# First modulation loaded alone, seven of eight cache samples compressed beside the projections: a prediction for one decoder step

## The chip, the cores and the metric

One core of one Trainium2 chip runs the whole program in one launch. The metric is device time in microseconds (us), the median of several executions. The engines are called PE (TensorE), DVE (VectorE), ACT (ScalarE), POOL (GpSimd) and SP (SyncE, which here only issues transfers). They run on their own and wait for one another by semaphores; each works through its own list of instructions in order.

## What is computed

One step of a hybrid decoder layer: 512 prompt tokens and 8 sampled tokens go through attention with three branches, a gated linear recurrence (HGRN) and a mixture of experts. What matters here is the start of the layer. A vector `c` per sequence gives six modulations, the input is normed and modulated, and projected:

```python
sh_a, sc_a, gt_a, sh_f, sc_f, gt_f = adaln(c, w_ada[l], b_ada[l])   # silu(c) @ w_ada + b_ada
h = rms_norm(x, g_pre_mix[l]) * (1.0 + sc_a) + sh_a
parts = split_projection(h @ w_in[l])
```

Each of the 8 samples also has a cache of 1024 rows in pages, found by a page table, which the compressed branch squeezes by a small two-layer network. That needs neither the modulation nor the projections:

```python
past_c = pool_c[page_table].reshape(b, past, NSA_KV_GROUPS, 2, NSA_HEAD_DIM)
hid = hid + jnp.einsum('bnsgkd,ksde->bngke', ch[:, r:r + n_cmp], w1r[:, r])
return jnp.einsum('bngke,kef->bngkf', jax.nn.gelu(hid), w2)
```

## The kernel before

The 520 tokens are columns of 128-row tiles; D = 1024 makes KT = 8 slices. Four pieces of work make up the start.

**The normed input.** `normed(t)` loads a tile of 128 tokens on ACT's queue, norms it on ACT and DVE, and transposes it on PE (L356) into `xnT`.

**The first modulation.** `ada(0, ...)` multiplies silu(c) (`sT`) with 8 slices of `wa`, each in two halves of 512 KB, L229, which SP loads into five tiles in turn (`mh0` to `mh3` and `wa`; the profile says `mh` and `wa`). Then it loads bias and gain (`bg`, L235), adds them on DVE (L237 and L240), and the caller transposes the result on PE (L378). ACT copies that (L379); ACT, DVE and POOL then make `hhi` and `hlo` from it slice by slice (L389 to L391), a pair of tiles that together hold the input for fp32r matmuls. Modulations 1 and 2 are made later by the same function, from loads of 1 MB (L223) into two tiles called `wa`, with sums in the bank `pf`.

**The compression.** `sample_compress()` handles one sample after another: 8 pages of 128 KB on SP's queue into a tile `cg` (three such tiles), 16 matmuls with `w1c` (L310), a GELU on ACT and DVE over `Bsc`, `hidc` and `huc`, and 4 matmuls with `w2c` (L325, L328) that give `KCS` and `VCS`.

**The projections.** `proj(ft)` makes one 128-row block of `h @ w_in` (L408): its weights `wr` are loaded on ACT's queue (ft 0 at L373, the rest at L398), split into `wh` and `wl` on ACT and DVE, and multiplied in 48 matmuls with `hhi` and `hlo`. Each attention block is copied by ACT to `kvt`, and six of them are stored by SP (L427). Ten such blocks and the gates (L472) are made; then the HGRN projections (L574) begin, with the attention rows (L657) among them and, between those, the attention of the samples, which starts with a small product at L750 that needs the table `s24`. At L215 SP also loads the other caches (`csk`, `csv`).

Strings set the order in which these pieces are written: in `ORD_A` x is a step of `all_normed`, a one of `ada(0)`, s one of the compression (two to a sample); in `ORD_B` n is a projection, s again the compression, a the modulations 1 and 2. A scheduler arranges each engine's instructions near that order. `play` goes through a string and finishes what is left.

Of the kernel before, what the change touches and what calls it, by code (L numbers as in the profile page):

```python
# [11 lines left out]
F32 = mybir.dt.float32  # L12
# [10 lines left out]
D = 1024  # L23
# [3 lines left out]
KT = 8  # L27
# [22 lines left out]
LOP = ()  # L50
NWA = 1
FIRST = 6
DMAN = False
NCG = 3

ORD_A = "xaxsaaxaxssssaaaxsassaaas"
ORD_B = "ssnaasnaanaanaanaasnaanaansnaannsnassnasaa"
ORD_C = "PPPrPsPrPPrPsPrPPsPrPPrPsPrPPrsPPPrPsPrPPrttsPPrPPrsPPPrsPPrPPrsPPrPsPPrPPrsPPrttPsPrPPrPsPPrPsPrPPrPsPrPPsPrPPrPsPrttPPrsPPrPPsPrPPrsPPrPPrsPPPrsPPPPsPPPsPPPPPPPPPtt"
# [8 lines left out]
def body(tc, I, O):  # L67
# [22 lines left out]
    def ps_mm():  # L90
        return bank("mm", 2, 512)
# [21 lines left out]
    def split(src, hi, lo, eng=None):  # L113
        act.activation(hi, src, AF.Copy)  # L114
        (eng or dve).tensor_tensor(lo, src, hi.bitcast(F32), op=ALU.subtract)  # L115
# [57 lines left out]
    def play(order, **gens):  # L173

        for c in order:
            next(gens[c], None)
        for g in gens.values():
            for _ in g:
                pass

    def steps(g, n):
        for _ in range(n):
            if next(g, self_end) is self_end:
                return
            yield
# [31 lines left out]

    def ada(gq, tiles, ps_1, mod):
        p = ps_1()
        for k in range(KT):  # L220
            if gq:
                w2 = tiles()
                sp.dma_start(w2, I["wa"][gq, k].rearrange("j p n -> p j n"))  # L223
            for j in range(2):
                if gq:
                    wa = w2[:, j]
                else:
                    wa = tiles()
                    sp.dma_start(wa, I["wa"][gq, k, j])  # L229
                for q in range(2):  # L230
                    r = slice(64 * j + 32 * q, 64 * j + 32 * q + 32)
                    pe.matmul(p[r, :], sT[:, k, :], wa[:, 512 * q:512 * q + 512], start=(k == 0), stop=(k == KT - 1))
            yield
        bg = (tiles()[:, 0] if gq else tiles()).rearrange("p (a b) -> p a b", a=2)
        sp.dma_start(bg, I["bg"][gq])  # L235
        mod = bg[:, 0] if mod is None else mod
# [49 lines left out]
    w1c = pc_.tile([128, 2, 8, 128], F32, name="w1c")  # L286
    sp.dma_start(w1c, I["wphi"])
    w2c = pc_.tile([64, 2, 64], F32, name="w2c")
    sp.dma_start(w2c, I["wphi2"])
    b1c = pc_.tile([64, 2], F32, name="b1c")  # L290
    sp.dma_start(b1c, I["b1"])
    cw = open_pool("cw", 1, s_cw)
    cq = open_pool("cq", 2, s_cw)

    def sample_compress():
        cgs = []

# [5 lines left out]
        for b in range(8):  # L303
            while len(cgs) < min(b + NCG, 8):
                load()
            cg = cgs[b]
            p = (ps_f if b % 2 and b < FIRST else ps_o)()
            for k in range(2):
# [55 lines left out]
    def all_normed():  # L364
        for t in range(5):
            normed(t)
            yield

    was = itertools.cycle([lambda c=c: mslot[c](F32, D) for c in range(4)] + [lambda: p0.tile([128, D], F32, name="wa", bufs=1)] * NWA)
    samples = sample_compress()  # L370
    play(ORD_A, x=all_normed(), a=ada(0, lambda: next(was)(), lambda: ps_mm()[:, 0], mod0), s=steps(samples, ORD_A.count("s")))
    wr0 = mslot[1](F32, KT, 128)
    act.dma_start(wr0, I["wi"][0])  # L373
    wi0 = [mslot[c](F32R, KT, 128) for c in (2, 3)]
    split(wr0, *wi0)
    pt = ps_t()
# [155 lines left out]

    def modulations():
        for gq in (1, 2):
            yield from ada(gq, lambda: wap.tile([128, 2, D], F32, name="wa", bufs=2), ps_f, None)

# [1518 lines left out]
```

## Time and profile before

| | us |
|---|---|
| median of three runs | 751.45 |
| lowest and highest | 748.72, 760.17 |
| the profiled execution | 756.68 |
| its span, from the first instruction to the last | 755.0 |
| PE busy in the span | 651.7 |
| DVE busy | 454.5 |
| ACT busy | 371.4 |

All views are of this one execution. Times in the trace count from the span's start. An engine letter with q (SPq, ACTq) is its queue, where it issues transfers; PEld is PE's weight load, which overlaps its matmuls. A matmul of fp32 shows as two records in the trace (16 matmuls of L310 are 32 records), one of fp32r as one.

### The profile page before, as it was taken

To read this page: it belongs to the slowest core of one execution; us is meant where nothing else is said; L and a number is where in the kernel's file an instruction comes from. 1 tells how busy PE (TensorE), PEld (TensorE's weight loads), DVE (VectorE), ACT (ScalarE), POOL (GpSimd) and SP (SyncE) were. 2 spreads that over 40 slices of the span, in tenths; PEclk is the share of its full clock that TensorE was granted. 3 is DMA by queue.
4 is the path that set the end of the run, shared out by engine and by line. 5 is a ranking of instruction groups with operands and counts; after the bars stand their busy time and mean duration, and the time that the engine had idled before them with its cause. 6 is when DMAs were issued, how large, how long until landed. Compare 5 with 4: busy or idle time off the path is not lost. (4 is left out here: it accounts for less than half of the span.)

```text
span 755.0 us, 13127 instructions
## 1 busy us (share of the span) xinstructions
PE 651.7 (86%) x4510; PEld 489.4 (65%) x4510; DVE 454.5 (60%) x1092; ACT 371.4 (49%) x770; POOL 152.0 (20%) x183
## 2 busy tenths in 40 slices
PE   3796799999899999989999989996779899999940
PEld 1663757679777868889776656564456577666620
DVE  4612623345684876557884453556886976888824
ACT  4311523323454454562454454436466757888833
POOL 1000310000231022140210131625211222222113
PEclk9988999999899999989999999999698999999985
DMA  8777599884545453510832356339899889998526
GB/s 292 255 255 237 185 345 315 306 269 148 182 150 156 139 172 122 187 33 27 311 128 79 112 192 182 127 117 342 280 381 330 248 220 310 348 328 297 158 31 226
DMA packets 74605, 160.83 MB, mean 213 GB/s; under 512 B 11346, under 2 KB 39538, under 8 KB 74146
## 3 DMA queue, kind: packets, MB, share of 16 engines
q1 hardware_dynamic: 59844, 125.98, 48.8%
q10 hardware_dynamic: 10654, 25.39, 10.0%
q0 software_dynamic: 4032, 8.53, 5.2%
q8 instruction: 38, 0.62, 0.4%
q14 instruction: 37, 0.30, 0.1%
HBM read 145.29 MB, written 24.28 MB: 225 GB/s over the span
## 5 line engine op out<-in xcount | busy, mean ns | idle before, releaser
L574 PE MATMUL pp<-hhi,wh 128*128 128x260 f32 x256 | 76.6, 299 | 0.3 <-ACT kvt L452 0.3
L574 PE MATMUL pp<-hlo,wh 128*128 128x260 f32 x256 | 75.4, 295 | 0.0
L574 PE MATMUL pp<-hhi,wl 128*128 128x260 f32 x256 | 75.4, 295 | 0.0
L574 PEld LDWEIGHTS pp<-hhi,wl 128*128 128x128 f32 x256 | 50.5, 197 | 2.8 <-issue 2.7
L574 PEld LDWEIGHTS pp<-hhi,wh 128*128 128x128 f32 x256 | 50.4, 197 | 2.6 <-issue 2.0
L574 PEld LDWEIGHTS pp<-hlo,wh 128*128 128x128 f32 x256 | 50.5, 197 | 1.2 <-issue 1.0
L1720 POOL DMA_INDIRECT Y<-ot,gi x17 | 24.4, 1437 | 131.1 <-ACT ot L1719 124.0
L666 ACT ACTIVATE jn<-P,M 128x128 bf16<-128x128 f32 (+3 forms) x64 | 35.9, 561 | 30.2 <-DVE M L664 24.9
L115 DVE TENSOR_TENSOR wl<-wr,wh 128x1024 fp32r<-128x1024 f32 x9 | 11.2, 1249 | 38.8 <-ACT wh L114 38.8
L1077 ACT ACTIVATE PT<-mm 128x256 f32<-128x256 f32 x80 | 24.2, 388 | 18.1 <-PE mm L1073 18.1
L664 DVE CUSTOM_DVE_ANT_0 P<-mm,tb 128x128 f32<-128x128 f32 (+3 forms) x64 | 29.0, 484 | 4.8 <-PE mm L657 4.8
L408 PE MATMUL mm<-hhi,wh 128*128 128x260 f32 x144 | 30.0, 288 | 1.3 <-ACT wh L114 1.3
L114 ACT ACTIVATE wh<-wr 128x1024 fp32r<-128x1024 f32 x9 | 9.5, 1056 | 41.8 <-PE mm L408 22.4
L1691 PE MATMUL pf<-ewi,xh 128*96 128x512 f32 x72 | 30.0, 416 | 0.0
L408 PE MATMUL mm<-hlo,wh 128*128 128x260 f32 x144 | 29.9, 285 | 0.0
L408 PE MATMUL mm<-hhi,wl 128*128 128x260 f32 x144 | 29.7, 287 | 0.0
L1691 PE MATMUL pf<-ewi,xl 128*96 128x512 f32 x72 | 29.0, 403 | 0.6 <-DVE xl L115 0.6
L657 PE MATMUL mm<-ka,qs 128*128 128x512 f32 (+2 forms) x112 | 27.7, 355 | 0.1
L310 PE MATMUL po<-cg,w1c 128*128 128x128 f32 x160 | 24.5, 313 | 2.8 <-DMA cg<-in_cc 2.8
L310 PEld LDWEIGHTS po<-cg,w1c 128*128 128x128 f32 x160 | 22.7, 224 | 6.6 <-issue 3.3
L1718 ACT ACTIVATE ot<-mm 96x512 f32<-96x512 f32 x17 | 10.1, 593 | 33.3 <-PE mm L1715 33.3
L1073 PE MATMUL mm<-qs,ka 128*128 128x512 f32 x80 | 25.7, 401 | 0.0
(657 smaller groups left out, 1840.6 us busy)
## 6 DMA issues: line engine op xcount, KB each, us to landing
ewr<-in_ew SPq DMA_DIRECT2D x37, 512.0 KB
wa<-in_wa SPq DMA_DIRECT2D x16, 1024.0 KB
wr<-in_wi ACTq DMA_DIRECT2D x25, 512.0 KB
ewt<-in_ew SPq DMA_DIRECT2D x24, 512.0 KB
cg<-in_cc SPq DMA_DIRECT2D x64, 128.0 KB
ewh<-in_ew SPq DMA_DIRECT2D x16, 512.0 KB
x<-in_ew SPq DMA_DIRECT2D x15, 512.0 KB
mh<-in_wa SPq DMA_DIRECT2D x13, 512.0 KB
```

The costliest lines, as they stand in the source:

```text
L115: (eng or dve).tensor_tensor(lo, src, hi.bitcast(F32), op=ALU.subtract)
L310: pe.matmul(p[:, 128 * k:128 * k + 128], w1c[:, k, s, :], cg[:, :, k, s, :], start=(s == 0), stop=(s == 7))
L408: pe.matmul(p[:, hf, 0:260], a[:, k, :], b[:, k, hf * 260:hf * 260 + 260], start=(k == 0 and j == 0), stop=(k == KT - 1 and j == 2))
L574: pe.matmul(p[:, 0:260], a[:, k, :], b[:, k, c], start=(k == 0 and j == 0), stop=(k == KT - 1 and j == 2))
L657: pe.matmul(o, QS[g][:, h % 4, qc], KA[g][:, j, a:b], start=(j == 0), stop=(j == 1))
L664: dve.tensor_tensor_reduce(out=p, in0=sb[:, br], in1=tb0[:, 384 - 128 * i:512].rearrange("p (k n) -> p k n", n=128), scale=SL[h], scalar=1 ...
L666: act.activation(jn[:, 0:128 * (i + 1)], p.rearrange("p k n -> p (k n)"), AF.Exp, scale=-1.0, bias=M[:, 0, i, br, h:h + 1], accum_out=M[:, ...
L1073: pe.matmul(S[:, br], KS[g][:, q, br, j], QS[g][:, :, qc], start=False, stop=(q == 1))
L1077: act.activation(PT[:, :, h], S4[:, :, h], AF.Exp, scale=-SL[4 * g + h])
L1691: pe.matmul(pg, a[:, k, :], b[:, wk_], start=(k == 0 and j == 0), stop=(k == 7 and j == 2))
L1718: act.activation(o3[:, 0], pd[:, 0], AF.Copy)
L1720: pool.indirect_dma_start(out=Y, out_offset=bass.IndirectOffsetOnAxis(ap=gix, axis=0), in_=ot, in_offset=None, bounds_check=T - 1, oob_is_ ...
```

## The change

The first modulation's weights come in 8 loads of 1 MB (a pair of halves each), into four tiles that get their proper content only later: `AK` and `AG` of the attention rows, `qs0` and `qs1` of the queries. Its bias has a tile of its own, `bg0`, loaded on ACT's queue; ft 0's weights `wr0` are loaded and split there too, with the last step of the normed input. `w1c`, `w2c`, `b1c` and the pages are loaded behind the weights. Modulations 1 and 2 load into four tiles in turn (`AK`, `AG` and the two of `wa`). In `ORD_A` only two steps of the compression are left, all behind the modulation; in `ORD_B` there are more, and the sums of all samples go to the bank `po` (before, three of them went to `pf`).

```diff
-NWA = 1
-FIRST = 6
-ORD_A = "xaxsaaxaxssssaaaxsassaaas"
-ORD_B = "ssnaasnaanaanaanaasnaanaansnaannsnassnasaa"
+ORD_A = "xaxaxaxaxaaaass"
+ORD_B = "nsasnasanasnasasnasnasansasnasanasnasasnanaa"
...
-    def ada(gq, tiles, ps_1, mod):
+    def ada(gq, tiles, ps_1, mod, bg=None):
...
-            if gq:
-                w2 = tiles()
-                sp.dma_start(w2, I["wa"][gq, k].rearrange("j p n -> p j n"))
+            w2 = tiles()
+            sp.dma_start(w2, I["wa"][gq, k].rearrange("j p n -> p j n"))
...
-                if gq:
-                    wa = w2[:, j]
-                else:
-                    wa = tiles()
-                    sp.dma_start(wa, I["wa"][gq, k, j])
+                wa = w2[:, j]
...
-        bg = (tiles()[:, 0] if gq else tiles()).rearrange("p (a b) -> p a b", a=2)
-        sp.dma_start(bg, I["bg"][gq])
+        if bg is None:
+            bg = tiles()[:, 0].rearrange("p (a b) -> p a b", a=2)
+            sp.dma_start(bg, I["bg"][gq])
...
-    sp.dma_start(w1c, I["wphi"])
...
     def sample_compress():
+        sp.dma_start(w1c, I["wphi"])
+        sp.dma_start(w2c, I["wphi2"])
+        sp.dma_start(b1c, I["b1"])
...
-            p = (ps_f if b % 2 and b < FIRST else ps_o)()
+            p = ps_o()
...
+        normed(4)
+        act.dma_start(wr0, I["wi"][0])
+        act.dma_start(bg0, I["bg"][0])
+        split(wr0, *wi0)
+        yield
...
+    two = [lambda n=n: wide(at1.tile([128, 2 * D], F32, name=n)) for n in ("AK", "AG")]
+    was = itertools.cycle(two + [lambda n=n: wide(nso.tile([128, 2 * D], F32, name=n)) for n in ("qs0", "qs1")])
...
     def modulations():
+        was = itertools.cycle(two + [lambda: wap.tile([128, 2, D], F32, name="wa", bufs=2)] * 2)
         for gq in (1, 2):
-            yield from ada(gq, lambda: wap.tile([128, 2, D], F32, name="wa", bufs=2), ps_f, None)
+            yield from ada(gq, lambda: next(was)(), ps_f, None)
```

PE's list, before, from the last weights of the first modulation to the first matmuls of ft 0 (L232 is the modulation, L310 the compression's first product, L325 and L328 its second, L378 the transposes of the modulation, L408 the projection):

```order
L232 MATMUL mm<-mh_617,sT 32x512 x2
L310 MATMUL pf<-cg,w1c 128x128 x7
L378 MATMUL pt<-ident,mod_140 128x128 x4
L325 MATMUL pt<-hidc,w2c 64x64 x2
L328 MATMUL pt<-w2c,hidc 64x64 x2
L310 MATMUL pf<-cg,w1c 128x128 x9
L310 MATMUL po<-cg,w1c 128x128
L408 MATMUL mm<-hhi,mh_756 128x260 x2
```

The same place in the changed kernel, whose lines are shifted by up to 7 (L225 is the modulation, L304, L319 and L322 the compression, L381 the transposes, L411 the projection):

```order
L225 MATMUL mm<-qs_336,sT 32x512 x4
L350 MATMUL pt<-ident,xin 128x8 x8
L225 MATMUL mm<-qs_342,sT 32x512 x4
L304 MATMUL po<-cg,w1c 128x128 x25
L319 MATMUL pt<-hidc,w2c 64x64 x2
L322 MATMUL pt<-w2c,hidc 64x64 x2
L381 MATMUL pt<-ident,mod_137 128x128 x4
L304 MATMUL po<-cg,w1c 128x128 x7
L411 MATMUL mm<-hhi,mh_148 128x260 x2
```

Before, samples 0 to 4 stand ahead of these rows, and 7 instructions of sample 5 ahead of the transposes. Now the transposes stand behind sample 0, 9 instructions of sample 1 and sample 0's second product.

SP's list before, at its start (all the rows are transfers but the two in which SP reads the page table):

```order
L283 DMA cT_119<-in_cT 128x256
L287 DMA w1c_123<-in_wphi 128x2048
L289 DMA w2c_125<-in_wphi2 64x128
L291 DMA b1c_127<-in_b1 64x2
L229 DMA mh0_179<-in_wa 128x1024
L229 DMA mh1_183<-in_wa 128x1024
L211 TENSOR_LOAD ptab_85
L215 ISA
L215 DMA cg_216<-in_cc 128x256
```

And in the changed kernel:

```order
L220 DMA AK_180<-in_wa 128x2x1024
L220 DMA AG_215<-in_wa 128x2x1024
L220 DMA qs0_250<-in_wa 128x2x1024
L220 DMA qs1_285<-in_wa 128x2x1024
L220 DMA AK_324<-in_wa 128x2x1024
L220 DMA AG_330<-in_wa 128x2x1024
L220 DMA qs0_336<-in_wa 128x2x1024
L220 DMA qs1_342<-in_wa 128x2x1024
L287 DMA w1c_123<-in_wphi 128x2048
L288 DMA w2c_124<-in_wphi2 64x128
L289 DMA b1c_125<-in_b1 64x2
L209 TENSOR_LOAD ptab_85
```

Before, 24 pages of three samples follow the first two weight loads. Now all pages follow the eight weight loads and `w1c`. In the part that follows, SP's stores of `kvt` stand between weight loads of modulations 1 and 2 and the pages of samples 4 to 7, and the table `s24` stands behind 8 pages of `csk`, where it stood behind 30.

## Rows read from the trace of the kernel before

**Rows 1.** The page: the span, PE's busy time, and in 40 equal slices PE's busy share and granted clock, in tenths.

```profile
span 755.0 us, 13127 instructions
PE 651.7 (86%) x4510; PEld 489.4 (65%) x4510; DVE 454.5 (60%) x1092; ACT 371.4 (49%) x770; POOL 152.0 (20%) x183
...
PEclk9988999999899999989999999999698999999985
```

**Rows 2.** Stretches of the span. Columns: from and to, length, busy us and number of instructions of each engine, granted clock as a share of full, mean busy share of the 16 DMA engines, GB/s moved.

```profile
core 0: us, PE busy (x) PEld busy (x) DVE busy (x) ACT busy (x) POOL busy (x), PEclk, DMA share, GB/s
...
0.00:4.00 4.00, 0.00 (x0) 0.00 (x0) 0.00 (x0) 1.22 (x1) 2.22 (x15) 1.00 0.42 132
...
4.00:12.00 8.00, 1.25 (x2) 0.18 (x2) 2.13 (x11) 2.78 (x6) 0.00 (x0) 1.00 1.02 392
...
19.00:60.00 41.00, 33.57 (x232) 25.59 (x232) 16.06 (x60) 10.48 (x31) 0.47 (x4) 0.88 0.77 252
...
60.00:75.50 15.50, 9.90 (x57) 5.34 (x55) 3.44 (x9) 1.63 (x5) 0.12 (x1) 0.78 0.76 240
...
72.00:76.00 4.00, 3.80 (x18) 3.54 (x18) 1.38 (x2) 0.00 (x0) 0.00 (x0) 0.54 0.86 274
...
75.50:93.80 18.30, 14.54 (x111) 13.92 (x110) 11.93 (x25) 10.45 (x20) 6.40 (x7) 0.90 0.56 177
...
92.00:132.00 40.00, 35.32 (x280) 25.52 (x278) 12.53 (x22) 12.88 (x21) 5.55 (x11) 1.00 0.95 336
...
93.80:188.80 95.00, 89.44 (x728) 70.28 (x728) 35.94 (x64) 29.50 (x54) 7.10 (x13) 1.00 0.81 278
```

**Rows 3.** Timeline of SP's queue around the bias of the first modulation. Columns: start, length of the merged issues, what is issued, how many.

```profile
64.75 3.96 SPq L215 DMA_DIRECT2D cg<-in_cc  x8
68.81 0.38 SPq L235 DMA_DIRECT2D mh<-in_bg  x1
```

**Rows 4.** Timeline of PE, ACT and DVE from 20 to 94 us. Columns: start, length, engine, line, operation, out<-in, shapes, records; in brackets the idle time just before and what ended it.

```profile
20.94 5.44 PE L310 MATMUL po<-cg,w1c 128*128 128x128 f32 x32 [2.82 <-DMA cg<-in_cc]
...
51.30 3.84 PE L310 MATMUL pf<-cg,w1c 128*128 128x128 f32 x32
...
54.97 1.95 PE L310 MATMUL po<-cg,w1c 128*128 128x128 f32 x16
55.26 0.27 ACT L317 ACTIVATE Bsc<-pf 64x128 f32<-64x128 f32 x1 [4.46 <-PE pf L310]
...
59.14 0.33 PE L325 MATMUL pt<-hidc,w2c 64*64 64x64 f32 x4 [0.82 <-DVE hidc L278]
...
59.64 0.49 PE L310 MATMUL po<-cg,w1c 128*128 128x128 f32 x2
...
72.20 3.33 PE L310 MATMUL pf<-cg,w1c 128*128 128x128 f32 x14 [4.04 <-DMA mh<-in_bg]
74.02 0.69 DVE L237 TENSOR_TENSOR mod<-mm,mh 128x512 f32<-128x512 f32 x1 [7.42 <-DMA mh<-in_bg]
...
75.49 0.71 PE L378 MATMUL pt<-ident,mod 128*128 128x128 f32 x4
...
77.73 0.80 ACT L389 ACTIVATE hhi<-xnT,modT 128x512 fp32r<-128x512 f32 x1
...
80.48 1.06 ACT L114 ACTIVATE mh<-mh 128x1024 fp32r<-128x1024 f32 x1 [1.95 <-DMA cg<-in_cc]
...
93.82 0.51 PE L408 MATMUL mm<-hhi,wh 128*128 128x260 f32 x2 [1.31 <-ACT wh L114]
```

**Rows 5.** Transfers issued in the first 215 us: out<-in, queue, operation, how many, KB each.

```profile
wa<-in_wa SPq DMA_DIRECT2D x16, 1024.0 KB
cg<-in_cc SPq DMA_DIRECT2D x64, 128.0 KB
...
xin<-in_xp ACTq DMA_DIRECT2D x4, 512.0 KB
...
w1c<-in_wphi SPq DMA_DIRECT2D x1, 1024.0 KB
```

**Rows 6.** PE's groups of instructions from 93.8 to 188.8 us. Columns: line, operation, names, shapes, records; busy us, mean ns of one; idle us just before and what ended it.

```profile
L232 PE MATMUL pf<-wa,sT 128*32 128x512 f32 x128 | 18.1, 604 | 5.3 <-DMA wa<-in_wa 5.1
...
L310 PE MATMUL po<-cg,w1c 128*128 128x128 f32 x32 | 3.7, 275 | 0.0
...
L325 PE MATMUL pt<-hidc,w2c 64*64 64x64 f32 x12 | 1.0, 242 | 0.0
```

**Rows 7.** PE's waits in the same stretch: who, line, for whom; us in total, times, longest.

```profile
PE pf L232 <- DMA wa<-in_wa: 5.1, 8, 1.4
PE mm L408 <- ACT wh L114: 1.3, 1, 1.3
```

**Rows 8.** PE's wait behind the projections, from the waits of 188 to 300 us, and five rows of its timeline there: the first HGRN matmul, two at the usual spacing, two behind the wait.

```profile
PE pt L750 <- DVE rg L747: 3.4, 1, 3.4
...
188.84 0.39 PE L574 MATMUL pp<-hhi,wh 128*128 128x260 f32 x1 [0.26 <-ACT kvt L452]
...
189.19 0.28 PE L574 MATMUL pp<-hhi,wl 128*128 128x260 f32 x1
189.31 0.28 PE L574 MATMUL pp<-hhi,wh 128*128 128x260 f32 x1
...
197.29 0.42 PE L574 MATMUL pp<-hhi,wh 128*128 128x260 f32 x1
197.51 0.42 PE L574 MATMUL pp<-hlo,wh 128*128 128x260 f32 x1
```

More of the change, by code (lines that the diff above doesn't have):

```diff
@@ L286, in body @@
     w1c = pc_.tile([128, 2, 8, 128], F32, name="w1c")
-    sp.dma_start(w1c, I["wphi"])
     w2c = pc_.tile([64, 2, 64], F32, name="w2c")
-    sp.dma_start(w2c, I["wphi2"])
     b1c = pc_.tile([64, 2], F32, name="b1c")
-    sp.dma_start(b1c, I["b1"])
     cw = open_pool("cw", 1, s_cw)
@@ L364, in all_normed, with wide @@
     def all_normed():
-        for t in range(5):
+        for t in range(4):
             normed(t)
             yield
-    was = itertools.cycle([lambda c=c: mslot[c](F32, D) for c in range(4)] + [lambda: p0.tile([128, D], F32, name="wa", bufs=1)] * NWA)
-    samples = sample_compress()
[L371 to L375, printed above, removed]
+        normed(4)
[3 more added lines that the diff above has]
+        yield
+    bg0 = p0.tile([128, 2, 512], F32, name="bg0")
+    wr0 = mslot[1](F32, KT, 128)
+    wi0 = [mslot[c](F32R, KT, 128) for c in (2, 3)]
+    def wide(t):
+        return t.rearrange("p (j n) -> p j n", j=2)
+    two = [lambda n=n: wide(at1.tile([128, 2 * D], F32, name=n)) for n in ("AK", "AG")]
+    was = itertools.cycle(two + [lambda n=n: wide(nso.tile([128, 2 * D], F32, name=n)) for n in ("qs0", "qs1")])
+    samples = sample_compress()
+    play(ORD_A, x=all_normed(), a=ada(0, lambda: next(was)(), lambda: ps_mm()[:, 0], mod0, bg0), s=steps(samples, ORD_A.count("s")))
     pt = ps_t()
```

## The prediction

> **What bounds the kernel now.** The page first [rows 1]: TensorE (PE) is busy 86% of a span of 755.0 us, so a stage in which PE has to wait is where time can be won, and work that is moved into a stage where PE is full costs its whole length there. The table by stretches [rows 2] shows which is which. Up to 75.5 us the kernel loads: 240 to 252 GB/s between 19 and 75.5 us, and the matmuls there follow what lands. From 93.8 to 188.8 us, the attention projections, PE is busy 89.4 of 95.0 us at full clock. The chain that ended last covers only the end of the program, so the boundary between the two is read from the timeline [rows 4]: the transposes of the first modulation (L378), for which every projection waits, start at 75.5 us, because bias bg, queued behind sample pages on SP's queue [rows 3], kept VectorE (DVE) from adding it until 74.0 us (7.4 us idle), and PE's next work, sample 5, waited until 72.2 us for its pages.
>
> So two questions decide: when do those transposes start now (I call it T), and what do the moved compressions cost behind them.
>
> **When T comes.** The changed order of PE and SP (shown with the change) says what stands ahead of it: all eight weight pairs, sample 0's compression, 9 of the 16 instructions of sample 1's and sample 0's second product. Bias bg0 and ft 0's weights now come on ACT's queue, out of the way.
>
> Loads. Eight pairs of 1.05 MB, four x tiles of 0.52, wi0 and bg0 of 0.52 each and 0.1 of cT make 11.7 MB (sizes as in [rows 5]). The first 4 us move 132 GB/s x 4 = 0.5 MB; the other 11.2 MB take 28.6 us at the 392 GB/s of 4 to 12 us or 33.3 us at the 336 of 92 to 132 us [rows 2]. So the last pair lands at 33 to 37 us. I take 36: the second row is the same 1 MB load, though with only two tiles in turn; here there are four. The reuse of a tile waits for PE's four matmuls on it, some 15 us ahead of need, and costs nothing; if that cover were gone, a load would start one matmul group (1 us) late.
>
> Sample 0's pages. w1c goes ahead of them, 1.05 MB or 3.1 us at 336 GB/s. The pages are issued at 0.5 us each (eight in 3.96 us, [rows 3]); some are issued behind w1c meanwhile, so the last goes out about 1.1 us after w1c, at +4.2 us. From the end of the last issue to the matmuls that wait for a set, sample 5 took 72.2 - 68.7 = 3.5 us [rows 3, 4]. So PE starts sample 0 at 36 + 7.7 = 43.7 us.
>
> Its 32 records (16 fp32 matmuls, two records each) took 5.4 us at 20.9 us after a wait, 3.8 us when PE had been working; 14 records at 72.2 took 3.3 us, at a granted clock of 0.54 over 72 to 76 us, which is 1.2 GHz most of the time [rows 2, 4]. By that row all 32 would take 7.6 us. I take 5.4, the row that also waited for sample 0's pages; ends 3.8 and 7.6. A rule bears on this: the Trainium skill, "TensorE: Matmul & The Clock Gate", section "Part 1: The HAM clock gate", says that the clock is halved by default and that activity releases it, so a PE made idle in the loading phase starts cold. The trace agrees (0.54 at 72 to 76 us). By the rule alone sample 0 would cost the 7.6 us and the result would be 2.2 us later.
>
> Then the chain from the sum in PSUM through ACT and DVE to the second product: 59.1 - 55.3 = 3.9 us, and the product itself 0.5 us [rows 4]. Sample 1's nine instructions (18 records, 2.1 us) fit in there: its last page goes out 4 us after sample 0's, so it is ready at 47.7, before sample 0's matmuls end at 49.1. T = 43.7 + 5.4 + 3.9 + 0.5 = 53.5 us, 22.0 us earlier than 75.5.
>
> **From T to the second projection (ft 1).** Before: 75.5 to 93.8, 18.3 us. In it ACT stood from 78.5 (end of the row at 77.73) to 80.5 us and then split ft 0's weights for 1.06 us, a load issued only at 75.5; both go, -3.0 us. The rest is the chain over eight slices of hhi and hlo, which stays, and about 2 us of PE work after it, which stays too (one weight pair of the second modulation and a piece of sample 2 for the half of sample 6). 15.3 us.
>
> **The projections, ft 1 to the start of the HGRN projections (L574 at 188.8).** Before 95.0 us. Added: L310 has 32 records there now (one sample, [rows 6]) and will have 184 (samples 3 to 7 and 12 instructions of sample 2): 152 x 0.115 us (51.30 to 54.97 for 32) = 17.4 us. Second products: 7 for 3, four times 0.5 = 2.0 us. One of the sixteen weight groups now runs ahead of ft 1: -1.05 us. Removed: PE's 5.1 us of waits for wa [rows 7], since four tiles instead of two hold these weights; bounds 0 and 5.1. New: each second product waits for its 3.9 us chain, with 17 to 48 matmuls of 0.12 us and often a 1.05 us weight group put between; where it is 17 to 24, up to 1 us is bare. 3 us in all, bounds 0 and 8; if the cover were gone it would be 7 x 3.9 = 27. Sum: 95.0 + 17.4 + 2.0 - 1.1 - 5.1 + 3 = 111.2 us.
>
> So the HGRN projections start at 53.5 + 15.3 + 111.2 = 180.0 us, 8.8 us earlier. Of 22.0 us won at T and 3.0 behind it, PE takes back 16.2.
>
> **Behind that.** PE waits 3.4 us at L750 for the small table s24, issued on SP behind 30 pages of csk, and then issues every 0.22 us instead of 0.12 for some 24 matmuls, 2.3 us more [rows 8]. In the changed order s24 stands behind 8 pages, so this wait should go; but the other 22 pages of csk then come later for the sample attention. I take 3 of 5.7 us, bounds 0 and 5.7. The rest of the program keeps its work and moves up by as much.
>
> Sum: 8.8 + 3 = 11.8 us off the profiled span of 755.0, 743.2. The median of the runs shown is 751.45 (748.72 to 760.17), the profiled run 756.68; so I forecast 751.45 - 11.8, about 740 us.
>
> **The rivals.**
> *A: more is won.* Loads at 392 GB/s (-3 us), sample 0 at 3.8 us (-1.6), no new waits for second products (-3), the whole stall at L750 gone (-2.7): 22 us, 729 us. For it: every piece has a row. Against: PE idles longer before sample 0 than it did before 51.3 us.
> *B, the other side: loading becomes the bound of the projections.* Between 75.5 and 188.8 us 18.3 x 0.177 + 95.0 x 0.278 = 29.6 MB were moved [rows 2]; now some 36 pages (4.7 MB) more come in it, less wi0: 33.8 MB in 15.3 + 111.2 = 126.5 us, 267 GB/s. The 336 of 92 to 132 us speaks against it; for it speak the 240 to 252 GB/s of the stretches with pages, and that SP issues in order: kvT stores, which wait for ACT, stand between wa loads and pages. At 240 GB/s it takes 141 us, 14 more: 754 us. It decides from 33.8 / (126.5 + 11.8) = 244 GB/s down: below that the change is slower.
> *C: nothing is won because T stays bound by bytes.* T would have to be at 65, that is weights landing at 47.5, 11.2 MB in 43.5 us or 257 GB/s. Possible only if four tiles in turn load no faster than the 252 of 19 to 60 us, which had pages among them; then 751 us.
>
> **How the numbers follow.** My forecast (4 to 19 us won, 732 to 747 us) 0.64, A 0.15, B 0.13, C 0.08. Over 2% (about what a measurement of this kernel can tell from no change) is 15 us: A and a third of the forecast's cases, 0.36. Slower by 2% needs B below 220 GB/s and is 0.06; the rest, 0.58, is within 2%. The range 730 to 752 takes in C, and leaves out half of A and most of B, together under 0.2.
>
> **What the profile will show.** Right: last modulation weights used near 37 us, L381 near 53, ft 1's first matmul near 69, L578 near 180, no wait of PE for wa, none for s24. T later than 58 says the pages or the cold clock cost more; waits of PE for cg or wa among the projections say B; waits for hidc say the covers were too thin. The forecast is wrong if T comes before 48 or after 60, or if the projections take 100 or 122 us.

## The result, and the profile after

| | before | after |
|---|---|---|
| median, us | 751.75 | 759.98 |
| lowest and highest, us | 748.72, 760.17 | 757.12, 768.91 |
| ratio to before, 95% interval | | 1.010 (1.0057 to 1.0142) |
| the profiled execution, its span, us | 756.68, 755.0 | 757.12, 755.3 |

The change makes the kernel about 1% slower; I had forecast 740 us and a range of 730 to 752. The ratios, here and below, leave out slow runs (over 1.5% above the kernel's fastest, as the 768.91 of after), which the medians and the highest values keep. By the ratio after is 7.5 us slower, by the medians 8.2. The two profiled spans are 0.3 us apart where the medians are 8 us apart: the execution of before that was profiled was 5 us over its median, that of after 3 us under its own. Executions of one kernel differ with the mean granted clock here (one kernel below took 753.9 us at 0.950 and 763.0 at 0.937), so one pair of profiles can't rank the kernels. Whatever follows is read from several.

The page of after: span, PE's busy time, granted clock.

```profile
span 755.3 us, 13098 instructions
...
PE 650.3 (86%) x4510; PEld 484.1 (64%) x4510; DVE 459.7 (61%) x1092; ACT 372.3 (49%) x770; POOL 155.6 (21%) x183
...
PEclk9879999999999999999999979997798999999985
```

PE is as busy as before [rows 1]. Stretches of after, columns as in [rows 2], cut at its own milestones:

```profile
4.00:32.00 28.00, 16.80 (x88) 6.01 (x88) 15.72 (x59) 9.45 (x17) 0.00 (x0) 0.95 1.03 411
32.00:52.50 20.50, 10.44 (x78) 9.02 (x74) 5.39 (x18) 3.32 (x8) 0.12 (x1) 0.73 0.70 215
...
67.90:182.10 114.20, 108.61 (x904) 90.30 (x904) 46.50 (x97) 38.97 (x87) 10.22 (x38) 0.99 0.75 259
182.10:350.90 168.80, 161.25 (x1328) 134.74 (x1329) 116.77 (x416) 80.12 (x205) 35.31 (x45) 0.99 0.41 128
...
434.30:446.00 11.70, 4.77 (x20) 4.02 (x21) 5.91 (x12) 7.07 (x11) 3.77 (x3) 0.70 0.78 255
```

The weights load at 411 GB/s (392 in [rows 2]), PE is busy 95% of the projections (108.6 of 114.2 us), and there is a hole at 434 to 446 us, with PE busy 4.8 of 11.7 us at a clock of 0.70. PE's timeline, columns as in [rows 4]: the last modulation matmuls, samples 0 and 1, the transposes, ft 1, the first HGRN matmul.

```profile
33.47 1.06 PE L225 MATMUL mm<-qs,sT 128*32 128x512 f32 x8
41.96 5.98 PE L304 MATMUL po<-cg,w1c 128*128 128x128 f32 x32 [7.43 <-DMA cg<-in_cc]
49.84 2.25 PE L304 MATMUL po<-cg,w1c 128*128 128x128 f32 x18 [1.90 <-ACT Bsc L311]
...
52.50 0.66 PE L381 MATMUL pt<-ident,mod 128*128 128x128 f32 x4
...
67.91 0.51 PE L411 MATMUL mm<-hhi,wh 128*128 128x260 f32 x2
...
182.11 0.39 PE L578 MATMUL pp<-hhi,wh 128*128 128x260 f32 x1 [0.69 <-ACT kvt L455]
```

So far the forecast holds: the transposes come 23 us earlier, the HGRN projections 6.7 us earlier than in [rows 8]. In this pair of profiles the lead is even 8.6 us at the first score matmul of the attention (358.0 for 366.6 us), and the first expert matmul (L1691 of before, L1695 of after) starts at 541.7 us in both. Of the 8.6 us, 3.8 are left at the first matmul of the output projection (442.3 for 446.1 us), and none by 457: from there to the experts both take 84.7 us. PE up to 457 us, before, then after:

```profile
446.00:457.00 11.00, 11.00 (x67) 7.04 (x67) 3.05 (x13) 1.10 (x3) 2.62 (x10) 1.00 0.87 281
```

```profile
442.30:457.00 14.70, 11.84 (x54) 6.70 (x56) 8.76 (x10) 1.41 (x3) 6.83 (x12) 0.76 0.91 314
```

So the lead is lost in the hole and in the 15 us behind it, where PE still waits and its granted clock is 0.76 for 1.00. After, in the hole, SP, ACT, PE and DVE (the lines are 4 higher than in before; L1351 is the router's transposes of the table `tab`, L1305 the output projection, L113 and L112 splits of its weights and inputs):

```profile
434.28 0.32 SPq L1384 DMA_DIRECT2D xr<-in_xs  x1
434.37 0.39 ACTq L1329 DMA_DIRECT2D tab<-MOD  x1
...
437.74 3.90 ACT L112 ACTIVATE ewh<-wq 128x1024 fp32r<-128x1024 f32 x4 [0.83 <-issue]
...
440.71 1.94 PE L1351 MATMUL pt<-ident,tab 128*128 128x128 f32 x8 [4.66 <-DMA tab<-MOD]
...
442.30 0.78 PE L1305 MATMUL mm<-ewh,mhh 128*128 128x512 f32 x1
442.69 0.69 DVE L633 COPY hT<-pt 128x512 f32<-128x512 f32 x1 [4.25 <-PE pt L1351]
443.29 6.87 DVE L113 TENSOR_TENSOR ewr<-wq,ewh 128x1024 fp32r<-128x1024 f32 x4
```

And before:

```profile
437.69 3.90 ACT L114 ACTIVATE ewh<-wq 128x1024 fp32r<-128x1024 f32 x4
...
438.80 4.63 DVE L115 TENSOR_TENSOR ewr<-wq,ewh 128x1024 fp32r<-128x1024 f32 x4
...
439.55 0.30 SPq L1380 DMA_DIRECT2D xr<-in_xs  x1
...
444.18 1.94 PE L1085 MATMUL po<-PT,VT 128*64 128x256 f32 x14
...
446.05 0.50 PE L1301 MATMUL mm<-ewh,mhh 128*128 128x512 f32 x1
...
456.33 1.09 PE L1347 MATMUL pt<-ident,tab 128*128 128x128 f32 x8
```

Before, the splits run beside the attention's last matmuls and the router's transposes stand behind the output projection's first tile. After, all of that starts behind the attention's last matmuls (433.9 us), the transposes come first, PE waits 4.7 us for their table and DVE with its splits behind them. None of these lines is in the diff: the scheduler set this stretch in another order. Two more things differ there that the diff doesn't name. `xr` leaves at 439.55 us before, as soon as the last score matmul (439.1) is done and 6 us ahead of the last value matmul; after, it leaves only when the value matmuls are through. And `xr` lies elsewhere in relation to the attention's tiles: a tile of the pool `nso` gets its address in the order in which names are first taken, `qs0` and `qs1` are now taken first (for weights), and what lay under `xr` is no longer `ka1`, which the scores read, but `VT`, which the value matmuls read. No row shows an address; the two times at which `xr` leaves agree with it, and part 3 tests it.

### The profile page after: what moved, and what is told of

Read it like the earlier page. It is cut to its first block, busy times and chain, and to the rows that moved or that the text cites. A ratio compares the mean times of both kernels' runs of the same rounds, so it can differ in the third digit from the quotient of the medians.

```text
span 755.3 us, 13098 instructions
## 1 busy us (share of the span) xinstructions
PE 650.3 (86%) x4510; PEld 484.1 (64%) x4510; DVE 459.7 (61%) x1092; ACT 372.3 (49%) x770; POOL 155.6 (21%) x183
## 3 DMA queue, kind: packets, MB, share of 16 engines
q10 hardware_dynamic: 10798, 25.91, 10.1%
## 5 line engine op out<-in xcount | busy, mean ns | idle before, releaser
L578 PE MATMUL pp<-hhi,wh 128*128 128x260 f32 x256 | 75.5, 295 | 0.7 <-ACT kvt L455 0.7
L578 PE MATMUL pp<-hlo,wh 128*128 128x260 f32 x256 | 73.8, 288 | 0.0
L304 PE MATMUL po<-cg,w1c 128*128 128x128 f32 x256 | 33.6, 290 | 10.6 <-DMA cg<-in_cc 7.4
L304 PEld LDWEIGHTS po<-cg,w1c 128*128 128x128 f32 x256 | 31.7, 203 | 16.1 <-DMA cg<-in_cc 8.3
L113 DVE TENSOR_TENSOR wl<-wr,wh 128x1024 fp32r<-128x1024 f32 x9 | 11.5, 1272 | 33.7 <-ACT wh L112 33.7
L411 PE MATMUL mm<-hhi,wh 128*128 128x260 f32 x144 | 31.6, 296 | 0.1
L1695 PE MATMUL pf<-ewi,xh 128*96 128x512 f32 x72 | 30.9, 430 | 0.0
L411 PE MATMUL mm<-hhi,wl 128*128 128x260 f32 x144 | 29.6, 287 | 0.3 <-DVE wl L113 0.3
L1695 PE MATMUL pf<-ewi,xl 128*96 128x512 f32 x72 | 29.7, 412 | 0.0
L411 PE MATMUL mm<-hlo,wh 128*128 128x260 f32 x144 | 29.6, 286 | 0.0
L411 PEld LDWEIGHTS mm<-hhi,wh 128*128 128x128 f32 x144 | 22.8, 192 | 6.1 <-issue 3.8
L1722 ACT ACTIVATE ot<-mm 96x512 f32<-96x512 f32 x17 | 10.1, 593 | 33.4 <-PE mm L1719 33.4
L1670 POOL DMA_INDIRECT XG<-H,gi x18 | 21.1, 1175 | 23.5 <-PE pt L1683 9.5
```

The source lines that it names most:

```text
L304: pe.matmul(p[:, 128 * k:128 * k + 128], w1c[:, k, s, :], cg[:, :, k, s, :], start=(s == 0), stop=(s == 7))
L411: pe.matmul(p[:, hf, 0:260], a[:, k, :], b[:, k, hf * 260:hf * 260 + 260], start=(k == 0 and j == 0), stop=(k == KT - 1 and j == 2))
L578: pe.matmul(p[:, 0:260], a[:, k, :], b[:, k, c], start=(k == 0 and j == 0), stop=(k == KT - 1 and j == 2))
L1670: pool.indirect_dma_start(out=xg, out_offset=None, in_=H2, in_offset=bass.IndirectOffsetOnAxis(ap=gix, axis=0), bounds_check=T - 1, oob_is ...
L1695: pe.matmul(pg, a[:, k, :], b[:, wk_], start=(k == 0 and j == 0), stop=(k == 7 and j == 2))
L1722: act.activation(o3[:, 0], pd[:, 0], AF.Copy)
```

## The experiments

**Reading them.** From the end of the attention projections on, both kernels write the same 3198 instructions, in the same sequence. So an order can be carried from one kernel to the other: `QUEUED` holds, for each engine, the places of its instructions in the sequence wanted, and each gets an edge to the one ahead of it (order alone, no wait).

```diff
+    first_at = len(nc.cur_bb.bb.instructions)
...
+    traced = nc.cur_bb.bb.instructions[first_at:]
+    for places in QUEUED:
+        for p, n in zip(places, places[1:]):
+            tc.add_manual_dep(traced[n], traced[p].name, mybir.DependencyInfo(mybir.DependencyClass.NoSync, mybir.DependencyReason.DATA), reason="order")
```

"Tail" is from the attention to the end of the output projections, "HGRN" the stretch ahead of it. The table has, for each profile, when the transposes and the HGRN projections start, how long the latter last (from the first to the last start of their matmuls), and the time from the first score matmul to the first expert matmul; then the time against the runs of before that were made beside it (a_all_s24 and c_best stand in the text).

| kernel | transposes | HGRN start | HGRN lasts | scores to experts | median | ratio (95%) |
|---|---|---|---|---|---|---|
| before | 75.5 | 188.8 | 170.7 | 175.1 | 751.75 | |
| b_again | 73.0 | 186.2 | 168.6 | 175.4 | 751.28 (one) | |
| b_layout | 76.4 | 185.3 | 163.7 | 183.6 | 754.61 | 1.0052 (1.0012 to 1.0091) |
| b_tail_as_after | 73.8 | 186.3 | 163.0 | 191.2 | 765.02 | 1.0213 (1.0154 to 1.0271) |
| b_s24 | 71.4 | 185.2 | 168.6 | 177.6 | 755.35 | 1.0042 (1.0019 to 1.0066) |
| b_hgrn | 69.5 | 187.7 | 183.5 | 175.9 | 769.1 | 1.0278 (1.0234 to 1.0321) |
| after | 52.5 | 182.1 | 168.8 | 183.7 | 759.98 | 1.010 (1.0057 to 1.0142) |
| a_again | 51.8 | 181.3 | 171.7 | 183.2 | 758.04 | 1.012 (1.0062 to 1.0179) |
| a_router_late | 53.9 | 182.3 | 172.1 | 181.4 | 760.73 | 1.0141 (1.0092 to 1.0191) |
| a_tail_as_before | 54.3 | 186.5 | 171.8 | 181.9 | 760.6 | 1.011 (1.0073 to 1.0147) |
| a_layout | 51.9 | 178.1 | 171.9 | 181.7 | 757.14 | 1.0089 (1.0053 to 1.0125) |
| a_layout_tail | 54.3 | 183.8 | 171.5 | 175.2 | 752.56 | 1.0002 (0.9963 to 1.0041) |
| a_all | 53.8 | 183.1 | 179.2 | 178.4 | 760.39 | 1.0123 (1.0082 to 1.0164) |
| c_early | 40.4 | 172.5 | 182.3 | 178.4 | 757.07 | 1.0099 (1.0071 to 1.0126) |
| c_tail | 40.6 | 172.9 | 182.7 | 180.4 | 759.22 | 1.0102 (1.0068 to 1.0136) |
| c_gather | 40.4 | 171.6 | 182.0 | 177.7 | 752.52 | 1.0012 (0.9982 to 1.0042) |
| c_best_s24 | 40.8 | 172.7 | 183.0 | 177.8 | 754.14 | 1.0019 (0.999 to 1.0049) |
| c_tables | 40.4 | 173.1 | 180.9 | 174.4 | 753.22 | 1.0013 (0.998 to 1.0045) |

**1. Again, and the tail's order in both directions.** a_again is the changed kernel. a_tail_as_before is the changed kernel with the tail's order of before in `QUEUED`, b_tail_as_after the reverse.

> The changed kernel once more, as the measure for the runs beside it. All theories: 757 to 761 us, tensor engine out of the attention at about 434 us and at the expert stage at about 541.7.

> The changed kernel, but from the attention to the end of the output projections every engine's queue holds its instructions in the order of the kernel before. Theory 'order' (the lead of 8 us is lost because the scheduler set this stretch in another order, in which the router's transposes and the splits of the output weights stand where they must wait): the lead of about 8 us reaches the expert stage, first matmul of it near 533 to 535 us, and the time falls by 6 to 9 us against the changed kernel, to 749 to 754. Rival 'bound' (the stretch waits for loads into memory that the attention frees, or for a chain elsewhere, in either order): expert stage at 540 to 542, time within 2 us of the changed kernel.

> The mirror of it: the kernel before, with the order of the changed kernel in every engine's queue from the attention to the end of the output projections; nothing of the change itself. Theory 'order': the stretch costs 6 to 9 us more, expert stage near 549 us, time 757 to 761 where the kernel before takes about 751. Rival 'bound': no change beyond 2 us.

a_again came as expected, its transposes and experts within 2 us of after's. The order alone, set back, brought 1.8 us in the tail and nothing in the time: "order" as the only cause falls. Put into before, it costs 16 us in the tail and 2.1% of the time, more than either theory allowed; PE waits 8.9 us for `tab` there. What a_tail_as_before still waits for shows in SP's queue, ACT's queue and PE's waits (one view each):

```profile
445.49 0.30 SPq L1391 DMA_DIRECT2D xr<-in_xs  x1
```

```profile
447.27 9.29 ACTq L1268 DMA_DIRECT2D Y<-zero  x5
```

```profile
PE pf L1329 <- ACT sns L1327: 4.2, 1, 4.2
```

Its last value matmuls start at 443.5 and end at 445.5: `xr` waits for them, and two loads of output weights and the first expert weight stand behind it on SP's queue. They leave 6 us later than in before and run beside the zeros that ACT writes to `Y`, whose five issues take 9.29 us (5.46 in before), and ACT, whose list goes on only behind them, is late for `sns`.

**2. The router's transposes alone.**

```diff
-        dve.tensor_tensor(cW[:, 0], router(GC...
+        with tc.issue_after(ahead[-1].ins):
+            dve.tensor_tensor(cW[:, 0], router(GC...
```

> The changed kernel with one place moved: the router's first eight transposes and its matmuls stand behind the first tile of the output projection on the tensor engine instead of ahead of it. Theory 'order' with the transposes as its whole cause (the 4.7 us that the tensor engine waits for the table, and the 4.3 us that the vector engine's copy behind them holds up the splits): 4 to 8 us less than the changed kernel. If ACT's splits of the weights, which start at 437.7 us behind the last exponentials, are the larger part: 1 to 3 us less, the first matmul of the output projection still near 442. Rival 'bound': no change beyond 1 us.

The output projection's first matmul still comes 8.3 us after the last value matmul starts (445.3 after 437.0 us), as ACT's splits, not the transposes, then hold it. 2.3 us less in the tail than after, the middle case; none in the time, as the rival had it.

**3. The addresses.** a_layout takes the five tiles ahead of the borrowed ones, a_layout_tail also has the tail's order of before, and b_layout gives before the addresses of after.

```diff
+    Vb = nso.tile([128, 2, 4, 64], F32, name="Vb")
+    VT = nso.tile([128, 4, 2, 128], F32, name="VT")
...
     two = [lambda n=n: wide(at1.tile([128, 2 * D], F32, name=n)) for n in ("AK", "AG")]
```

```diff
+    for n in ("qs0", "qs1"):
+        pool.memset(nso.tile([128, 4, NP], F32R, name=n)[:, 0, 0:1].bitcast(F32), 0.0)
     Vb = nso.tile([128, 2, 4, 64], F32, name="Vb")
```

> The changed kernel, with the tiles Vb, VT, ka0, ka1 and GT of the pool nso taken ahead of the first modulation, so that every tile of that pool has the address that it had in the kernel before (in the changed kernel qs0 and qs1, borrowed for weights, are taken first and push the others up, and the tile xr, whose loads stand ahead of the output weights' on SP's queue, then lies over VT, which the last attention matmuls read, where it lay over ka1, which only the scores read). The queues' order stays that of the changed kernel. Theory 'addresses alone': 6 to 9 us less than the changed kernel, 750 to 753. Theory 'order and addresses, each a part': the loads of xr and of the output weights leave 2 to 3 us earlier, but the tensor engine still waits for the table ahead of the output projection: 0 to 4 us less, 755 to 759. Theory 'lead not there' (the 8.5 us were a cold clock in the profiled run of before, and after is no earlier at the attention in truth): as the first of the two others, but the gap to the kernel before can't close.

> As a_layout, and the order of every engine's queue from the attention to the end of the output projections set to that of the kernel before: all that the change does behind its own stretch is undone. Theory 'order and addresses': from the first score matmul to the first expert matmul as before, about 176 us (175.1 in the profiled run of before, 183.7 in that of the changed kernel, 181.9 with the order alone set back), and the time 7 to 9 us under the changed kernel, 750 to 753; if the lead of 8 us was real, 744 to 748, under the kernel before. Theory 'lead not there': equal to the kernel before within 3 us, 749 to 754. If neither order nor addresses is the cause: 757 to 762.

> The kernel before, with two tiles qs0 and qs1 taken first in the pool nso (one column of zeros is written into each), so that its tiles have the addresses of the changed kernel; the order of its queues stays its own. Theory 'order and addresses': the loads of xr, two of the output weights and the first expert weight leave at about 445.5 us in place of 439.5, and the second half of the output projection waits some 4 us, as with the order alone set back: 754 to 757. Theory 'addresses alone': 757 to 760. Rival 'addresses cost nothing': 750 to 752.

> The kernel before once more, for its trace: its recorded profile took 756.7 us, where its other runs took 746 to 756, most near 751. Theory 'lead not there': the HGRN projections end near 350 to 354 us in place of 359.5, since the clock is not low at 190 to 210, 230 and 320 us, and the expert stage starts near 536. Otherwise: 541 as recorded.

In a_layout, with the addresses of before and the order of after, `xr` leaves right behind the last score matmul (430.3 us) again, where in after it left behind the last value matmul:

```profile
430.69 0.32 SPq L1385 DMA_DIRECT2D xr<-in_xs  x1
```

That is the sign the account by addresses needs. PE still waits 4.6 us for `tab` there, the tail is 181.7 us, and the time 757.14: the middle theory. In a_layout_tail `xr` leaves between the scores and the value matmuls, as in before, and the zeros take their 5.45 us; in b_layout, whose queues have their own order, it leaves with the end of the value matmuls, and the wait for `sns` is there. a_layout_tail, SP's queue; b_layout, SP's queue and PE's waits:

```profile
435.87 0.30 SPq L1392 DMA_DIRECT2D xr<-in_xs  x1
```

```profile
437.28 0.30 SPq L1382 DMA_DIRECT2D xr<-in_xs  x1
```

```profile
PE pf L1320 <- ACT sns L1318: 3.9, 1, 3.9
```

So the tail takes 175 us with both as in before, and 182 to 184 with either or both as in after (191 in b_tail_as_after): the two don't add up, each alone is enough. With both undone the kernel is level with before. This settles that the loss of 8 us arises in the tail; it also says that the lead isn't there: it would have put a_layout_tail 4 to 8 us below before. In time b_layout pays only 0.5%, though its tail is 8 us longer: its HGRN stretch is 5 us shorter than b_again's (163.7 for 168.6, and 163.0 in b_tail_as_after; the mean granted clock there was 0.99 for 0.97), which no edit of mine explains. b_again shows one reason for the missing lead. Its HGRN projections end at 354.8 us, where the recorded before had 359.5: 2.6 us of that lie ahead of the stretch and 2.1 in it, at a mean granted clock of 0.97 for 0.95. The single slices don't sort that way as I expected (0.76 and 0.74 in before at 190 to 200 and 320 to 330 us, 0.83 and 0.66 in b_again). Over the kernels with before's own front and order the end lies at 349.0 to 359.5 (mean 353.3), over those with the changed front and its own order at 350.0 to 358.3 (mean 353.7). HGRN starts 4 us earlier and lasts 4.4 longer.

**4. The HGRN stretch.** a_all: a_layout_tail with HGRN's order of before too, so that only the front differs. b_hgrn: the reverse, before with HGRN's order of after (both through `QUEUED`). c_early is a_all with the front shortened:

```diff
-ORD_A = "xaxaxaxaxaaaass"
-ORD_B = "nsasnasanasnasasnasnasansasnasanasnasasnanaa"
+ORD_A = "xaxaxaxaxaaaa"
+ORD_B = "nsssasnasanasnasasnasnasansasnasanasnasasnanaa"
```

> As a_layout_tail, with the order of the HGRN projections' stretch as well set to that of the kernel before: from the end of the first attention's projections on, every queue's order and every address is that of the kernel before, and only the change's own stretch is left. Theory 'second order': in the changed kernel the scheduler sets the samples' score matmuls of 32 columns (L830, L834) apart, between full-width ones, so that four of them no longer run side by side on the tensor engine: 16.0 us busy in place of 10.1 for the same 48 matmuls, and the HGRN stretch takes 171.5 to 172.1 us in place of 163.0 to 168.6. With the order of before it falls to 163 to 168, and the time to 745 to 749, 3 to 8 us under a_layout_tail and under the kernel before. Rival: the HGRN stretch is as long for another reason (the clock, what is left of the loads): 751 to 754, as a_layout_tail.

> The mirror: the kernel before, its own addresses and its own order of the tail, but the order of the changed kernel in the HGRN projections' stretch. Theory 'second order': the 48 score matmuls take about 16 us, the stretch 168 to 173 us, and the time is 754 to 758. Rival: 750 to 753.

> a_all with samples 0 and 1 taken out of the order ahead of the first modulation's transposes and put behind the first projection (in ORD_A the two s go, ORD_B begins with nsss): nothing stands between the last modulation matmul (33.5 us) and the transposes but the bias and its chain. All theories: transposes at 37 to 40 us in place of 52 to 54. If the tensor engine bounds the projections: HGRN start 8 to 12 us earlier than in a_all, 171 to 176 us, and 736 to 742 us in all. If the bytes do (the samples' pages and the modulations' rows at 340 to 390 GB/s): HGRN start within 4 us of a_all's, and 743 to 749.

The observation behind it holds: the samples' score matmuls take 10.1 us side by side and 15 to 16 apart. PE's groups of the HGRN stretch in b_again, then in after (columns as in [rows 6]):

```profile
L826 PE MATMUL pt<-mh,qb 128*32 128x512 f32 x32 | 5.9, 600 | 0.0
...
L830 PE MATMUL pt<-wnp,qb 128*32 128x512 f32 x16 | 4.2, 603 | 0.0
```

```profile
L830 PE MATMUL pt<-mh,qb 128*32 128x512 f32 x32 | 8.0, 600 | 0.0
...
L834 PE MATMUL pt<-wnp,qb 128*32 128x512 f32 x16 | 7.0, 605 | 0.5 <-ACT wnp L812 0.5
```

One takes 600 ns in either; the busy time counts overlaps once, so it tells how many ran together. (The Trainium skill, "TensorEngine Tiling (Array Packing)", section "Key Properties", says that different tiles of the array can work in parallel. The rows agree, and add that others between them end that.) But a_all, with 10.1 us, lasted 179.2 us, not 163 to 168, and c_early, which starts 14 us earlier than before, ends where the others end (354.8 us). b_hgrn has the score matmuls apart (16.5 us) and waits besides (5.5 us for `rg`, 2.8 for pages), so its 183.5 us prove nothing either. My theory fell as the whole cause. DVE's waits and SP's queue in c_early show what stood in the way:

```profile
DVE rg L759 <- DMA s<-in_s: 16.8, 1, 16.8
```

```profile
171.09 0.51 SPq L247 DMA_DIRECT2D MOD<-AG  x1
...
175.44 12.76 SPq L219 DMA_DIRECT2D mh<-in_csk  x22
...
190.62 0.45 SPq L755 DMA_DIRECT2D s<-in_s  x1
```

The store of the last modulation (`MOD`) and 22 page loads at 0.58 us each are issued ahead of the small table. Neither moves up with the transposes: the store leaves at 171.1 us as in before, the pages 3 us later.

**5. Is that queue the gate?** a_all_s24, b_s24 and c_best_s24 load `s24` at the program's start on ACT's queue (into a_all, before with its own order in `QUEUED`, and c_early); c_best is c_early once more. c_tables also moves the other five tables ahead of the 22 pages in SP's list. c_tail is c_early with the scheduler's own HGRN order, and c_gather that with the score matmuls of each result put together on PE (one output copy also moves on SP's queue).

```diff
+    s24 = cst.tile([24, 35], F32, name="s24")
+    act.dma_start(s24, I["s24"])
...
-    s24 = sa.tile([24, 35], F32, name="s24")
-    sp.dma_start(s24, I["s24"])
```

> As a_all, but the small table s24 (24 x 35) is loaded at the program's start on ACT's queue into a tile of its own, in place of on SP's queue behind 22 page loads of the samples. In a_all the HGRN stretch took 179.2 us: the vector engine's rg waited for s24, whose load left at 191.6, and the tensor engine for rg (6.2 us, with a clock of 0.66 and 0.56 behind it). Theory 'fixed gate' (with an earlier HGRN start the order of before only runs into a load that does not move up): the wait for rg is gone, the stretch takes 166 to 172 us, the time is 747 to 753. Rival: the next load of that queue takes its place (the pages csk and csv): the stretch stays at 175 to 179, 756 to 760.

> The kernel before, every queue in its own order behind the first attention's projections, with the same early load of s24. Theory 'fixed gate': its wait for rg (3.4 us in the recorded profile) goes, 746 to 750. Rival: it costs nothing there, 750 to 752.

> c_early once more, one look: HGRN start 172 to 173, the wait for rg 15 to 17 us, 754 to 758.

> c_early without the order of before in the HGRN stretch (the scheduler's own order there, which puts the matmuls on s24 and rg later), with the addresses and the order of the tail of the kernel before. Theory 'fixed gate': no wait for rg, HGRN start at 172 to 174; its score matmuls stand as far apart as in the changed kernel, so the stretch takes 171 to 177 us: 741 to 747. Rival: the loads of the stretch hold the tensor engine wherever they stand, HGRN end near 353: 750 to 755.

> c_tail with 24 matmuls of one queue moved: in the HGRN stretch the four score matmuls of 32 columns that fill one 128-row result (samples' L830 and L834 of the changed kernel) stand next to each other on the tensor engine, where c_tail's order has up to 153 others between them; everything else keeps c_tail's order (one copy of an output, out_sw, goes earlier on SP's queue). Theory 'side by side': their busy time falls from 20.8 us (14.5 and 6.3) to 10 to 11, as in the kernel before, the HGRN stretch from 182.7 to 171 to 175 us, and the time from 759 to 748 to 752. Rival: they fill time in which the tensor engine would wait for the pages anyway, and the waits grow by as much: stretch 179 to 183, 756 to 760.

> c_early with the early load of s24: the projections' lead of 13 us, the order of before in the HGRN stretch and in the tail with its score matmuls side by side, and no wait for rg. Theory 'order, addresses and the fixed gate are all that holds the lead back': HGRN start 172 to 174, stretch 166 to 173, expert stage near 523 to 529, 736 to 744 us, under the kernel before. Rival: the samples' pages, which follow on the same queue, bound the stretch wherever it starts: HGRN end near 353 as in all runs so far, 749 to 755.

> c_best_s24 with the five other tables of the sample attention (ts, tw, tcs, gm, jj) issued on SP's queue ahead of the samples' 22 page loads instead of behind them. In c_best_s24 the vector engine waited 13.8 us for tcs, whose load left at 189.8, and the tensor engine 12.7 us for what stood behind. Theory 'fixed gate' (the lead is held by what SP's queue issues late, not by the bytes): that wait falls under 2 us, HGRN start 172 to 174, stretch 167 to 173 us, end 340 to 346, time 738 to 746, under the kernel before. Rival 'pages': the samples' pages behind them then hold the tensor engine (waits for csk or csv of 8 us and more), HGRN end 350 to 356, 750 to 755.

c_best took 758.01 us; PE waits 16.1 us for `rg` as in c_early, but its HGRN projections end at 361.1 us. a_all_s24 came to 754.1 us, 1.0009 (0.9975 to 1.0044), 6 us under a_all: the late table was a cost there. In b_s24 it wasn't; the wait for `rg` fell only from 3.4 to 2.4 us, a wait for pages rose from 1.1 to 3.1, and the time by 0.4%, which I can't explain (that `QUEUED` costs nothing by itself was not tried). In the early kernels the wait moves along the same queue. DVE's waits in c_best_s24, then ACT's in c_tables:

```profile
DVE pcs L785 <- DMA tcs<-in_tcs: 13.8, 1, 13.8
```

```profile
ACT wnp L820 <- DMA wnp<-in_cw: 16.6, 4, 15.2
```

First `s24`, then `tcs`, then `wnp`, which stands last, behind the pages: all three times PE stops for 13 to 16 us and the stretch ends at 354 to 356 us (361 in c_best). So with before's order and the early start SP's queue holds the stretch, shown three times. With the scheduler's order (c_tail) no single wait of PE for another engine's work or a load is over 2.6 us, the score matmuls stand furthest apart (14.5 and 6.3 us), and it ends at 355.6. c_gather's groups:

```profile
L843 PE MATMUL pt<-mh,qb 128*32 128x512 f32 x32 | 8.9, 756 | 5.8 <-DMA mh<-in_csk 5.8
L847 PE MATMUL pt<-wnp,qb 128*32 128x512 f32 x16 | 4.7, 605 | 0.6 <-ACT wnp L825 0.6
```

Their busy time falls by 7 us and the median by 6.7, but in the profiles HGRN is only 0.7 us shorter: PE now waits 5.8 us for the pages. (Its tail, in the same order, is 2.7 us shorter, which is more.) That is the rival in the stretch and the theory in the time, so it doesn't tell. No version beat before.

## Why the prediction was wrong

**When T comes: right.** 53.5 us predicted, 52.5 found, 51.8 to 54.3 in the other kernels of the table with this front. The weights were faster than I took them (last matmul on them at 33.5, loads taken to end at 36), sample 0's pages slower (its matmuls 8.5 us behind, not 7.7), its matmuls 6.0 us for 5.4, at a low clock as feared (0.62 over 41.9 to 48 us). The 1.0 us that is left is a balance of these errors. (That sample 5's wait up to 72.2 us was for its pages, from which I took the time behind the last issue, was my reading; the row in [rows 4] puts it down to the bias, issued right behind them.)

**T to ft 1: right.** 15.3 predicted, 15.4 found.

**The projections: right in kind, 3.0 us too small.** 111.2 predicted, 114.2 found. Two terms were mis-sized and nearly cancel: of the wait for `wa` I removed all 5.1 us, and 3.8 stayed; the 3 us of bare waits for second products didn't come (PE waits for no `hidc`). The other 2.2 us are spread: PE is busy 108.6 us where the terms give 107.7, and some short waits. PE's longest, 67.9 to 182.1 us:

```profile
PE pf L225 <- DMA wa<-in_wa: 3.8, 2, 2.8
```

**The lead of 8.8 us at the HGRN start** was 6.7 in the profiles and 4 on the mean: 182.5 us over seven kernels with this front, 186.6 over six with the old one. (a_all_s24, whose one profile is of an execution of 763.4 us, is not in these means; its start was 190.6.) The profiled before, with its start at 188.8, was the latest of the six, and I measured every gain from it. I also took the gain from the median of 751.45, though the profiled execution that gave it was 5 us slower.

**Behind that: failed.** The wait for `s24` went, as I wrote. But I took a gain of 3 us for the stretch, and it lasts 171.3 us on the mean of the six kernels with its own order, where five of before's take 166.9. The lead at its start is only in part one for the samples' attention: SP issues many of its loads behind the last modulation's store. Before, then after, SP's queue:

```profile
171.07 0.34 SPq L247 DMA_DIRECT2D MOD<-wa  x1
172.18 15.30 SPq L215 DMA_DIRECT2D mh<-in_csk  x22
...
194.72 2.71 SPq L807 DMA_DIRECT2D wnp<-in_cw  x4
```

```profile
180.55 0.35 SPq L241 DMA_DIRECT2D MOD<-AG  x1
181.10 11.94 SPq L213 DMA_DIRECT2D mh<-in_csk  x18
...
193.13 1.80 SPq L811 DMA_DIRECT2D wnp<-in_cw  x4
```

The store is 9.5 us later than before and `wnp` only 1.6 earlier. But that this sets the end in the changed kernel's own order doesn't show: PE waits there 0.5 us for `wnp` and for no page. What grows is PE's busy time. Before, then a_again, the HGRN stretch (columns as in [rows 2]):

```profile
188.80:359.50 170.70, 160.31 (x1329) 139.23 (x1330) 116.86 (x419) 81.52 (x213) 35.33 (x66) 0.95 0.42 129
```

```profile
181.30:353.00 171.70, 164.47 (x1328) 137.38 (x1329) 116.40 (x416) 80.07 (x205) 34.52 (x45) 0.97 0.40 126
```

Over the six and the five kernels above PE is busy 163.9 us for 157.0 and idle 7.4 for 10.0; the score matmuls set apart (15.5 us for 10.1) are 5.4 of the 6.9. The mean granted clock is the same (0.97 in both). So the traces put most of the longer stretch down to them. That putting them together would win it back isn't shown: where I did so (a_all, a_all_s24, c_gather), PE waited longer for loads, and that part stays open.

**"The rest of the program keeps its work and moves up by as much": the step that failed most.** It keeps its work, but neither its order nor its addresses. Scores to experts took 183.5 us on the mean of two profiles for 175.3, and a_layout_tail gives back all of it with both undone. The sum by what was found: 4.1 won at the HGRN start, 4.4 lost in that stretch, 8.2 in the tail, 8.5 us slower; measured 8.2 by the medians, 7.5 by the ratio. That they agree so closely is in part luck: the HGRN starts alone lie 8 us apart (178.1 to 186.5). None of the signs that I had set for being wrong came, since all of them lie ahead of the HGRN projections.

No rival had the mechanism. C gave 751 us by transposes at 65 us and B 754 by waits in the projections, neither of which came; B's wait for `wa` is the one that was there in small.

## What to carry to other kernels

Where a scheduler and pools stand behind a change, its reach doesn't end where its diff ends: compare order and addresses of the whole program, above all where a load goes into memory that others free. A tile borrowed early moves its pool's other tiles, and a load over one of them may then wait for a later reader. A lead is worth only as much as the last queue that moves up with it, and a difference under 1% needs more than one profile of each kernel.

## What the hardware showed that I had not expected

Four matmuls of 32 columns that fill one result ran side by side in these traces only when they stood next to one another on PE's list: 48 records of 600 ns each took 10.1 us together, 15.0 in after and 20.8 in c_tail.

Five writes of zeros took 5.46 us of ACT's queue when the loads beside them had left 8 us earlier, and 9.29 (a_tail_as_before) and 10.05 (b_layout) when these left within 2 us: it looks as if transfers of one queue slow the issuing on another, and with it the engine whose list that is. No run moved these loads alone. Before:

```profile
447.94 5.46 ACTq L1257 DMA_DIRECT2D Y<-zero  x5
```
